# Where the weights and the token columns start in their rows: other start columns, and 258 + 256 in place of 256 + 258

## The chip, the cores and the metric

The kernel runs on one core of a Trainium2 chip. The metric is the time of one execution on the device, in microseconds (us); lower is better. Before the change three runs took 1018.99, 1019.06 and 1020.0 us, so the median is 1019.06 us.

A core has a matrix engine (TensorE, PE in the profile; PEld is its loading of weights), VectorE (DVE), ScalarE (ACT), GpSimd (POOL) and DMA queues, most of them fed by SyncE (SP). They run side by side and wait for one another by semaphores. Operands lie in a memory of 128 partitions; a "column" below is one fp32 value, 4 bytes, in every partition's row. TensorE accumulates in a memory of its own, which VectorE and ScalarE read.

## The reference

528 tokens (16 meta tokens and 512 real ones) of width 2048 are normalised, projected once into 65 tiles of 128 columns, and these feed two branches: a recurrence of 16 heads (r, k, v, a gate g, and two low-rank inputs), and a short gated convolution (B, C, h, a gate gc). The branches' outputs go through one output projection, the residual is added, and the result is normalised. In outline:

```python
hn = _rmsnorm(h_res, norm_in_g[l])
P = hn @ w_in[l]                                   # (528, 8320)
Pr, Pc = P[..., :RW_COLS], P[..., RW_COLS:]
prev = jnp.pad(Pr[:, :-1], ((0, 0), (1, 0), (0, 0)))
Pr = Pr + (prev - Pr) * mu_shift[l]                # token shift
r, k, v, g_r = ...                                 # 1024 columns each, then wl, al: 64 each
y = _rwkv7_recurrence(r, decay, k, v, kk, kk * a)
y_a = (groupnorm(y) + bonus) * jax.nn.silu(g_r)
Bg, Cg, hc, g_c = ...                              # 1024 columns each
y_b = Bg * _causal_depthwise_conv(Cg * hc, conv_w[l]) * jax.nn.silu(g_c)
h_res = h_res + jnp.concatenate([y_a, y_b], axis=-1) @ w_out[l]
out = _rmsnorm(h_res, norm_f_g)[:, N_META:]
```

The meta tokens are dropped at the end. So r and g_r, whose values are needed for the 512 real tokens but shifted by one, and C and h, which a convolution of width 3 reads, are needed for the real tokens and one or two before them; B and g_c for the real tokens alone; k and v for all 528.

## The kernel before

**The input projection.** The normalised input lies transposed in memory, in 16 rows of 576 columns each (`LX`), one row for every 128 of the 2048 input features; token t is at column t of a row. Each fp32 value is stored as a high part (`xh`) and a low part (`xl`), and the product is made of three matmuls: high weights times high x, high weights times low x, low weights times high x. For each of the 65 output tiles (8 each of k, v, r, g, C, h, B, gc, and one of the low-rank inputs, lora) the function `main` takes the weights in four quarters. A quarter holds four blocks of 128 x 128, and `steps` runs over the pieces of the token columns, the four blocks and the three products. Each matmul (line 326) has its own load of weights.

**The pieces.** Three constants say which token columns a tile computes: `FULL` (0 to 256 and 256 to 528; k, v, lora), `TAIL` (from 14, 514 columns in two pieces; r, g, C, h) and `REAL` (16 to 528 in one piece of 512; B, gc). So a tile of the first two kinds has 16 x 2 x 3 = 96 matmuls and one of the third 48. Each piece has a bank of the accumulator; `scaled` (line 345) copies it out on VectorE, multiplied by the tokens' scale, piece by piece.

**The weights' buffers.** A quarter of weights, 512 columns, comes by DMA, and `split_w` makes its high part (ScalarE, line 138) and low part (VectorE or GpSimd, line 139). They go into one of six buffers of 1088 columns: the high part begins at column `SHIFT[kind]`, the low part 512 columns behind it. The buffers are 17 x 64 columns long and the rows of x 9 x 64, so a start column's place within 64 columns is the same in every buffer and row.

**The order.** TensorE's order is written out by hand: a generator (`mains`) yields the projection's matmuls with an assumed duration of 0.43 ns a column, and the recurrence's preparation, inversion and steps call `fill` to put a given time's worth of them between their own small matmuls. Other engines are ordered by a scheduler. Until about 850 us TensorE works on the projection with the recurrence's work in between; behind it comes the output projection, seven products of a fast matrix multiplication (lines 1231 and 1433), with weights at column 40 of the same buffers or in places of their own.

Of the kernel before, what the change touches and what calls it, by code (L numbers as in the profile page):

```python
# [23 lines left out]
L = SEQ + META  # L24
# [50 lines left out]


LX = 576
SHIFT = {"lora": 16, "k": 16, "v": 32, "r": 30, "C": 30, "h": 62, "B": 16, "g": 30, "gc": 0, "out": 40}


@with_exitstack
def hymba_kernel(ctx: ExitStack, tc: tile.TileContext, xt, xtok, front, w_in, w_out, pv, lup, cst, msk, gf, out):
# [45 lines left out]
    def parts_of(kind, name):  # L128
        t = wp.tile([P, 2 * 512 + 64], F32R, tag="hl", name=name, bufs=6)
        o = SHIFT[kind]  # L130
        return t[:, o : o + 512], t[:, o + 512 : o + 1024]
# [45 lines left out]
    def tm(name):  # L177
        return tp.tile([P, LP], F32, tag="tm", name=name, bufs=3)
# [118 lines left out]
    with tc.issue_after(head):  # L297
        nc.vector.tensor_scalar(
            out=omm, in0=pvt[:, V_MU : V_MU + 33], scalar1=-1.0, scalar2=1.0, op0=ALU.mult, op1=ALU.add
        )  # L300
        for d, off in (
# [4 lines left out]
                out=d, in0=pvt[:, off : off + 8], scalar1=0.5, scalar2=None, op0=ALU.mult  # L306
            )
        nc.vector.tensor_scalar(
            out=hv[:, 4], in0=pvt[:, V_KA : V_KA + 8], scalar1=-0.5, scalar2=1.0, op0=ALU.mult, op1=ALU.add
# [1 line left out]

    nc.scalar.copy(ones, cs[:, C_BM : C_BM + P + 2])
    FULL = ((0, 256), (256, L))
    TAIL = ((14, 270), (270, L))
    REAL = ((META, L),)

    def steps(ps, ranges, k4, q, ks=range(4), rs_=range(2)):
# [13 lines left out]
    def banks(ranges, name, pool, tag):  # L331
        return [pool.tile([P, b - a], F32, tag=tag, name=f"ps_{name}_{r}") for r, (a, b) in enumerate(ranges)]

    def main(j, ranges, name):
        prefetch(2 * j + 4)
        ps = banks(ranges, name, pm, "main")
        for k4 in range(4):
            if k4 == 1:
                prefetch(2 * j + 5)
            yield from steps(ps, ranges, k4, 4 * j + k4)  # L340
        return ps

    def scaled(ranges, ps, dst, base):
        for (a, b), p in zip(ranges, ps):
            nc.vector.tensor_tensor(out=dst[:, a - base : b - base], in0=p, in1=rs[:, a:b], op=ALU.mult)
# [12 lines left out]
    def shift_real(ps, m, name, dst):  # L358
        pr = tp.tile([P, L + 1], F32, tag="pr", name=f"pr_{name}", bufs=2)
        scaled(TAIL, ps, pr, 14)  # L360
        sh = tm(f"sh_{name}")[:, 0:SEQ]
# [26 lines left out]
    def behind_of(what):  # L388
        return tc.issue_after(state.pop(what)) if what in state else nullcontext()

    def use(what, i, ps):
# [14 lines left out]
        elif what == "C":  # L406
            u = tm(f"u{i}")
            scaled(TAIL, ps, u, 14)
            got[what, i] = u
        elif what == "h":  # L410
            u = got["C", i]
            hh = tm(f"hh{i}")
            with behind_of("turned"):
                scaled(TAIL, ps, hh, 14)
            n = SEQ + 2
# [56 lines left out]
    def mains():  # L472
        pa = banks(FULL, "lora", pm, "main")
        pb = banks(FULL, "k0", pz, "tz")
        pc = banks(TAIL, "r0", pm, "main")
        pd = [pi.tile([P, SEQ], F32, tag="ser", name="ps_B0")]
        four = ((pa, FULL), (pb, FULL), (pc, TAIL), (pd, REAL))
        for k in range(4):
# [29 lines left out]
        for j in range(4, len(plan)):  # L508
            what, i = plan[j]
            rg = FULL if what in ("k", "v") else REAL if what in ("B", "gc") else TAIL  # L510
            ps = yield from main(j, rg, f"{what}{i}")
# [695 lines left out]
    def here(t, n):  # L1207
        return xa[t][:, n * 512 : (n + 1) * 512] if n < 2 else xb[n - 2][:, t]
# [147 lines left out]
    for u, unit in enumerate(units):  # L1356
        half, prod, g = unit
# [53 lines left out]
    with tc.manual_schedule(engines={mybir.EngineType.DVE, mybir.EngineType.Activation, mybir.EngineType.Pool}):  # L1411
# [16 lines left out]
        for part in range(2):  # L1428
# [7 lines left out]
            h = here(1, 2)[:, cols]  # L1436
# [70 lines left out]
```

## Time and profile before

| | |
|---|---|
| median of three runs | 1019.06 us |
| the profiled execution | 1019.06 us |
| its span, first to last instruction | 1017.3 us |
| TensorE busy | 1003.7 us, 9723 matmuls |
| VectorE / ScalarE / GpSimd busy | 675.5 / 393.5 / 270.6 us |
| mean granted clock of TensorE | 0.997 |

The page of the profile gives each engine's busy time and the chain of work that ended last, followed back from the last instruction. "Busy" for TensorE counts overlapping matmuls once: a matmul's own duration (some 0.28 us for 256 columns) is longer than the distance to the next one's start, since they are pipelined. The pace is therefore read from starts, or from the length of a long uninterrupted row of the chain, not from the durations. A row of the timeline has the start, the length, the engine, the line, what is written and read, the shape and the count.

### The profile page before, as it was taken

The numbers are of one execution on the slowest core, as the hardware profiler recorded it, in microseconds if no ns is written. First come the engines' busy times: TensorE is split into PE (matmuls) and PEld (weight loads), VectorE is DVE, ScalarE is ACT, GpSimd is POOL, SyncE is SP. The second block draws the span as 40 slices with busy tenths as digits, with TensorE's granted clock in tenths as the row PEclk, the third lists the DMA queues.
The fourth block names the chain that finished last, engine by engine and source line by source line (L and its number), as shares of the span: only waits on it lengthen the run. The fifth ranks groups of instructions, "written<-read, shape, count | busy, mean of one in ns | idle before, by whom it ended". The sixth has DMA issues, their size and how long they took to land.

```text
span 1017.3 us, 23682 instructions
## 1 busy us (share of the span) xinstructions
PE 1003.7 (99%) x9723; PEld 921.5 (91%) x9723; DVE 675.5 (66%) x1239; ACT 393.5 (39%) x729; POOL 270.6 (27%) x292
## 2 busy tenths in 40 slices
PE   9999999999999999999999999999999999999996
PEld 8999998999998999998999998889889898787875
DVE  7786855588665669554668553244555697998787
ACT  7553423344313434322434323222222335445453
POOL 0122514223123323222323222123332332015001
PEclk9999999999999999999999999999999999999998
DMA  9426485546665264853264746877663687695744
GB/s 324 152 82 152 134 210 147 149 124 164 163 158 164 91 168 104 211 148 117 85 178 108 200 139 185 295 224 226 222 206 94 186 272 193 171 327 134 177 124 166
DMA packets 185036, 174.82 MB, mean 172 GB/s; under 512 B 121568, under 2 KB 142816, under 8 KB 184416
## 3 DMA queue, kind: packets, MB, share of 16 engines
q1 hardware_dynamic: 182336, 164.40, 55.4%
q0 software_dynamic: 2304, 8.39, 4.7%
q8 instruction: 76, 1.25, 0.5%
q10 hardware_dynamic: 288, 0.52, 0.1%
q14 instruction: 32, 0.26, 0.1%
HBM read 136.92 MB, written 36.35 MB: 170 GB/s over the span
## 4 chain that ended last, share of the span: by engine, by line
PE 84%; DVE 9%; DMA 3%; issue 2%; ACT 1%; SPq 0%; POOL 0%; DVEq 0%; ACTq 0%; POOLq 0%
PE ps_v L326 9%; PE ps_g L326 9%; PE ps_k L326 9%; PE ps_h L326 9%; PE ps_r L326 9%; PE ps_B L326 9%; PE ps_gc L326 8%; PE ps_C L326 8%; DVE o L1204 3%; DMA wo<-in_w_out_dram 2%; PE g L671 2%; PE M L1231 2%; PE ps_lora L326 1%; PE zs L996 1%; PE zy L1000 1%
## 5 line engine op out<-in xcount | busy, mean ns | idle before, releaser
L138 ACT CAST w<-wr 128x512 fp32r<-128x512 f32 x252 | 153.3, 619 | 304.0 <-PE ps_C L326 53.0
L139 POOL TENSOR_TENSOR w<-wr,w 128x512 fp32r<-128x512 f32 x119 | 159.6, 1342 | 380.9 <-ACT w L138 315.6
L139 DVE TENSOR_TENSOR w<-wr,w 128x512 fp32r<-128x512 f32 x133 | 96.7, 733 | 112.2 <-ACT w L138 101.9
L326 PE MATMUL ps_v<-xh,w 128*128 128x272 f32 (+1 forms) x512 | 96.8, 286 | 0.0
L326 PE MATMUL ps_r<-xh,w 128*128 128x256 f32 (+1 forms) x512 | 96.7, 283 | 0.0
L326 PE MATMUL ps_h<-xh,w 128*128 128x258 f32 (+1 forms) x512 | 96.4, 285 | 0.0
L326 PE MATMUL ps_k<-xh,w 128*128 128x256 f32 (+1 forms) x512 | 95.7, 284 | 0.0
L326 PE MATMUL ps_C<-xh,w 128*128 128x258 f32 (+1 forms) x512 | 95.0, 284 | 0.0
L326 PE MATMUL ps_g<-xh,w 128*128 128x258 f32 (+1 forms) x512 | 93.5, 283 | 0.0
L326 PE MATMUL ps_B<-xh,w 128*128 128x512 f32 x256 | 83.4, 394 | 0.0
L326 PE MATMUL ps_gc<-xh,w 128*128 128x512 f32 x256 | 82.2, 396 | 0.2 <-DVE w L139 0.2
L326 PEld LDWEIGHTS ps_h<-xh,w 128*128 128x128 f32 x512 | 80.2, 189 | 1.1 <-issue 0.4
L326 PEld LDWEIGHTS ps_r<-xh,w 128*128 128x128 f32 x512 | 80.9, 189 | 0.3
L326 PEld LDWEIGHTS ps_v<-xh,w 128*128 128x128 f32 x512 | 80.3, 188 | 0.3
L326 PEld LDWEIGHTS ps_k<-xh,w 128*128 128x128 f32 x512 | 80.0, 189 | 0.5
L326 PEld LDWEIGHTS ps_C<-xh,w 128*128 128x128 f32 x512 | 79.9, 189 | 0.6
L326 PEld LDWEIGHTS ps_g<-xh,w 128*128 128x128 f32 x512 | 79.5, 189 | 0.3
L326 PE MATMUL ps_v<-xl,w 128*128 128x256 f32 (+1 forms) x256 | 73.1, 286 | 0.0
L326 PE MATMUL ps_h<-xl,w 128*128 128x256 f32 (+1 forms) x256 | 72.4, 283 | 0.3 <-issue 0.3
L326 PE MATMUL ps_k<-xl,w 128*128 128x256 f32 (+1 forms) x256 | 72.6, 283 | 0.0
L326 PE MATMUL ps_r<-xl,w 128*128 128x256 f32 (+1 forms) x256 | 72.5, 283 | 0.0
L326 PE MATMUL ps_g<-xl,w 128*128 128x256 f32 (+1 forms) x256 | 72.5, 283 | 0.0
(321 smaller groups left out, 2267.6 us busy)
## 6 DMA issues: line engine op xcount, KB each, us to landing
wr<-in_w_in_dram SPq DMA_DIRECT2D x126, 512.0 KB
ct<-opd SPq DMA_DIRECT2D x64, 288.0 KB
wo<-in_w_out_dram SPq DMA_DIRECT2D x24, 512.0 KB
x<-in_w_out_dram POOLq DMA_DIRECT2D x16, 512.0 KB, 6.0
opd<-ar SPq DMA_DIRECT2D x8, 576.0 KB
opd<-gt SPq DMA_DIRECT2D x16, 288.0 KB
opd<-bt SPq DMA_DIRECT2D x64, 64.0 KB
x<-in_w_out_dram SPq DMA_DIRECT2D x8, 512.0 KB
```

The source lines that it names most:

```text
L138: nc.scalar.copy(hi, rq)
L139: low[q] = eng.tensor_tensor(out=lo, in0=rq, in1=hi.bitcast(F32), op=ALU.subtract).ins
L326: nc.tensor.matmul(ps[r], ww[:, w], xx[:, kt, a:b], start=(kt == 0 and n == 0), stop=(kt == KT - 1 and n == 2))
L671: nc.tensor.matmul(z[h][:, c - c0], bk[hs, c, h : h + 2, :].rearrange("p a s -> p (a s)"), ar[hs, c].rearrange("p a s -> p (a s)"), start= ...
L996: nc.tensor.matmul(d[hs, j], w, x[hs], start=(a == 0), stop=(a == b - 1))
L1000: nc.tensor.matmul(d[ho, j], t[hs, o : o + CH], x[hs], start=(a == 0), stop=(a == b - 1))
L1204: nc.vector.tensor_tensor(out=lo, in0=rq, in1=hi.bitcast(F32), op=ALU.subtract)
L1231: nc.tensor.matmul(bank[s], left(prod, jj, m, s), w, start=(jj == 0 and n == 0), stop=(jj == 7 and n == 2))
```

## The change

Two constants change. The table of start columns, and the split of the 514 token columns:

```diff
-SHIFT = {"lora": 16, "k": 16, "v": 32, "r": 30, "C": 30, "h": 62, "B": 16, "g": 30, "gc": 0, "out": 40}
+SHIFT = {"lora": 16, "k": 16, "v": 16, "r": 32, "C": 64, "h": 32, "B": 16, "g": 32, "gc": 16, "out": 40}
...
     FULL = ((0, 256), (256, L))
-    TAIL = ((14, 270), (270, L))
+    TAIL = ((14, 272), (272, L))
     REAL = ((META, L),)
```

The weights of v move to column 16, where k's are; those of gc to 16, where B's are; those of r, g and h to 32; those of C to 64. For r, g, C and h the first piece is 14 to 272 (258 columns) and the second 272 to 528 (256 columns). What is computed, and the count of all instructions, stay the same.

## Prediction

> **What bounds the kernel now.** I read the page first (busy time per engine, then the chain that ended last), then the engines stage by stage, then what TensorE waits for, and last the chain and the timeline of single tiles, because the change touches only where TensorE reads. The page's busy times and its chain:
>
> ```profile
> span 1017.3 us, 23682 instructions
> PE 1003.7 (99%) x9723; PEld 921.5 (91%) x9723; DVE 675.5 (66%) x1239; ACT 393.5 (39%) x729; POOL 270.6 (27%) x292
> PE 84%; DVE 9%; DMA 3%; issue 2%; ACT 1%; SPq 0%; POOL 0%; DVEq 0%; ACTq 0%; POOLq 0%
> ```
>
> TensorE is busy for 99% of the span and carries 84% of the chain. Busy matmuls overlap, so this alone does not say that it is the limit. The view of stages (length, busy time and count for each engine, TensorE clock, DMA share, GB/s) and the view of TensorE's own waits say it:
>
> ```profile
> 0.00:53.00 53.00, 51.32 (x354) 46.47 (x355) 38.16 (x79) 33.45 (x66) 4.83 (x21) 1.00 0.70 235
> 53.00:150.00 97.00, 97.00 (x827) 95.43 (x826) 69.57 (x153) 40.54 (x75) 30.83 (x35) 1.00 0.55 143
> 700.00:850.00 150.00, 149.70 (x2002) 134.00 (x1998) 92.59 (x143) 45.76 (x85) 49.67 (x40) 1.00 0.68 202
> 850.00:1017.00 167.00, 156.05 (x698) 126.73 (x697) 143.83 (x208) 87.57 (x159) 28.50 (x30) 0.98 0.65 182
> ```
>
> ```profile
> PE M L1231 <- DVE o L1204: 1.7, 4, 0.7
> PE pwarm L187 <- DVE cold L184: 1.4, 1, 1.4
> PE rz L944 <- DMA ct<-opd: 0.2, 1, 0.2
> PE ps_gc L326 <- DVE w L139: 0.2, 1, 0.2
> ```
>
> From 53 to 850 us TensorE has no idle time worth a microsecond, at a granted clock of 1.00. Only behind 850 us, in the output projection, do 11 us stand open, and its VectorE is busy for 144 of 167 us. So a shorter input matmul (line 326) moves everything behind it forward, one for one, as long as the splits of the weights stay hidden. They do: TensorE waited 0.2 us for one of them, while ScalarE's cast, the first half of a split, waits for TensorE to free a buffer (columns: busy, mean ns of one, idle before it and what ended most of that):
>
> ```profile
> L138 ACT CAST w<-wr 128x512 fp32r<-128x512 f32 x252 | 153.3, 619 | 304.0 <-PE ps_C L326 53.0
> ```
>
> **How the pace depends on the column.** One tile is 96 matmuls in two pieces (k, v, r, g, C, h), or 48 in one piece of 512 (B, gc). The chain shows tiles that ran without interruption (start, length, count):
>
> ```profile
> 386.76 11.77 PE ps_v L326 x96
> 425.22 11.51 PE ps_C L326 x96
> 474.63 11.54 PE ps_k L326 x96
> 805.50 11.51 PE ps_C L326 x96
> 817.01 11.57 PE ps_h L326 x96
> 828.58 10.88 PE ps_B L326 x48
> 839.47 11.00 PE ps_gc L326 x48
> ```
>
> k and v read the same x columns (0 to 256 and 256 to 528), have equal counts and shapes, and differ in where the weights start in their buffer: column 16 against 32. The v tile takes 0.23 us more. B and gc both read x from column 16 in pieces of 512, with weights at 16 and at 0: gc takes 0.12 us more. So the position of the weights against x costs time, and it does so in the same way in buffers and rows whose bases differ by multiples of 64 columns (C takes 11.51 us at 425 and at 805 us).
>
> C has weights at 30 and x from 14 and from 270. Its 514 columns are 14 fewer than k's 528, yet it is only 0.03 us a tile faster. The timeline shows its two pieces beside k's. A low-half row (xl) stands for every third matmul, so the first to the fourth of a piece is nine matmuls:
>
> ```profile
> 477.45 0.28 PE L326 MATMUL ps_k<-xl,w 128*128 128x256 f32 x1
> 478.51 0.28 PE L326 MATMUL ps_k<-xl,w 128*128 128x256 f32 x1
> 478.87 0.28 PE L326 MATMUL ps_k<-xl,w 128*128 128x272 f32 x1
> 479.98 0.29 PE L326 MATMUL ps_k<-xl,w 128*128 128x272 f32 x1
> ```
>
> ```profile
> 428.05 0.28 PE L326 MATMUL ps_C<-xl,w 128*128 128x256 f32 x1
> 429.13 0.28 PE L326 MATMUL ps_C<-xl,w 128*128 128x256 f32 x1
> 429.49 0.28 PE L326 MATMUL ps_C<-xl,w 128*128 128x258 f32 x1
> 430.57 0.28 PE L326 MATMUL ps_C<-xl,w 128*128 128x258 f32 x1
> ```
>
> ```profile
> 819.86 0.28 PE L326 MATMUL ps_h<-xl,w 128*128 128x256 f32 x1
> 820.95 0.28 PE L326 MATMUL ps_h<-xl,w 128*128 128x256 f32 x1
> 821.30 0.29 PE L326 MATMUL ps_h<-xl,w 128*128 128x258 f32 x1
> 822.39 0.28 PE L326 MATMUL ps_h<-xl,w 128*128 128x258 f32 x1
> ```
>
> k: 1.06 / 9 = 117.8 ns for 256 columns and 1.11 / 9 = 123.3 ns for 272, so 16 columns cost 5.5 ns, about 0.35 ns each. C: 120.0 ns for 256 and 120.0 for 258. h: 121.1 and 121.1. Starts are given to 0.01 us, so a pace is good to about 1 ns. The same 256 columns are 2.2 ns dearer from column 14 (weights at 30) than from column 0 (weights at 16), though the distance, 16 columns, is equal: x that starts off a multiple of 16 costs something too.
>
> **The change part by part.** No instruction is added or removed, no DMA, no wait, no queue order. Buffers keep their 1088 columns (C's low half now ends at 64 + 1024, the last of them).
>
> (a) v from 32 to 16: exactly k's arrangement. 8 tiles x (11.77 - 11.54) = **-1.8 us**. The best known of the parts: the two rows differ in nothing else.
>
> (b) gc from 0 to 16: exactly B's arrangement. 8 x (11.00 - 10.88) = **-1.0 us**.
>
> (c) The second piece of r, g, C and h now reads x from 272, a multiple of 16, 256 columns instead of 258. For r, g and h the weights stand at 32, whose distance modulo 64 (272 is 16 more than a multiple of 64) is 16, which is k's first piece: 117.8 ns. r and g had C's arrangement, so C's 120.0 ns is taken for them: 48 matmuls x 8 tiles x 2.2 ns = 0.85 us each; h had 121.1: 384 x 3.3 = 1.27 us. For C the weights at 64 stand 48 columns from x modulo 64, which is gc's old place against x (0 against 16), the poor one of the two by the rows of gc and B. I take no gain there. Together 0.85 + 0.85 + 1.27 = **-3.0 us**. Bounds: no gain at all, and all four at 117.8, which is 3 x 0.85 + 1.27 = 3.8 us.
>
> (d) The first piece still starts at 14, with 258 columns, and weights at 32 (C: 64) instead of 30 (h: 62). No row shows weights on a multiple of 16 with x off it. What answers best for x is today's second piece (258 columns from 270, which is 14 modulo 64): 120.0 with weights at 30. From below the nearest row is k's 117.8, with two columns more, 118.5 ns. From above: position alone makes a difference of 2.4 ns a matmul between k and v (0.23 us / 96) and of 2.5 ns between B and gc (0.12 us / 48); that on top of 120.0 is 122.5. I take 119.3, between the lower end and today's second piece, because its x keeps that piece's place while the weights come to stand on a multiple of 16, as k's do. r, g and C: 384 x 3 x 0.7 = 0.8 us; h: 384 x 1.8 = 0.7 us. Together **-1.5 us**; bounds 1536 x (118.5 - 120.3) = -2.8 and 1536 x 2.2 = +3.4 us (120.3 being the mean of three at 120.0 and one at 121.1).
>
> (e) VectorE's scaling out of the accumulators takes 258 and then 256 columns instead of the reverse. The sum of the two is the same. The casts and subtractions write at other columns of the same buffer; they are hidden as shown above, and if one took some tens of ns longer it would cost nothing, for the buffer was freed several quarters earlier.
>
> (f) The order of TensorE's work is cut by a running sum of 0.43 ns a column. A first piece now counts 12 x 2 x 0.43 = 10 ns more and the second 10 ns less; a cut moves by one matmul at most. No wait is named above that stands within that distance; cost 0, and if it met the 0.2 us wait for a split, 0.2 us.
>
> Sum: 1.8 + 1.0 + 3.0 + 1.5 = 7.3 us. The profiled execution took 1019.06 us (span 1017.3 and 1.8 around it), which is the median of the three runs. 1019.1 - 7.3 = **1011.8 us**. What comes next to bind, behind 850 us, begins earlier by the same amount.
>
> [...]
>
> **The rivals.**
>
> Rival 1: column 32 is a dear column in itself, whatever x does. For it: v at 32 is dearer than k at 16 in both its pieces. Then r, g and h trade their 2.2 ns for v's 2.4 ns and gain nothing; only (a), (b) and a little of C and h remain: 1019.1 - 1.8 - 1.0 - 0.4 = 1015.9 us. Against it: with x from 14, weights at 30 pay 2.2 and weights at 62 pay 3.3 ns over k at 256 columns, so x off a multiple of 16 has a price at more than one column of the weights, and (c) takes it away.
>
> Rival 2, the other side: in the first piece, weights on a multiple of 16 and x 2 columns short of one meet in the same memory on every group of columns. Place: 1536 first-piece matmuls. It turns the whole change slower when it takes back the 5.8 us of (a) to (c) and 2 us more: 7.8 / 1536 = 5.1 ns a matmul, a pace of 125.4 ns. At 127 ns, say, the time is 1019.1 - 5.8 + 1536 x 6.7 / 1000 = 1023.6 us. For it: no row has this pairing, and gc shows that a mere shift can cost. Against it: the largest differences that position alone makes in the rows are the 2.4 and 2.5 ns above.
>
> Rival 3: the position of weights is not the cause, and v and gc are slower for another reason (their place in the order, what VectorE and GpSimd do beside them). Then nothing moves: 1019 us. Against it: gc and B, and C and h, ran back to back from 805 to 850 us under the same conditions and keep their difference. [...]
>
> **How the numbers follow.** The forecast, with (c) paying and (d) anywhere in its bounds: 0.66, from 1019.1 - 5.8 - 2.8 = 1010.5 (with C's second piece at 117.8 too, 1009.7) to 1019.1 - 5.8 + 3.4 = 1016.7 us. A further 0.06 goes to a larger gain than any row shows, down to 1006. Rival 1: 0.13. Rival 3: 0.07. Rival 2: 0.08. A difference under 0.2%, 2 us, can hardly be told from none; the three runs before spread over 1.0 us. Faster by more than that takes the forecast, the larger gain and most of rival 1 (1015.9 is 3.2 us): 0.66 + 0.06 + 0.11 = 0.83. Within: rival 3 and the rest of rival 1, 0.09. Slower: 0.08. From 1007 to 1017.5 us the range leaves out rivals 2 and 3 and the far end of the larger gain, 2 in 10.
>
> **What would show it.** In the chain of the changed kernel an uninterrupted v tile should take 11.54 us and a gc tile 10.88. In the timeline the 256-column piece of r, g and h should run at 117 to 118 ns and C's at about 120; the 258-column piece at 118.5 to 120. The stage from 53 to 850 us should show no new idle time of TensorE, and the projection's start should move forward by about 7 us. Wrong would be: a 258-column piece above 122 ns, v still at 11.77 us, or an equally early projection that ends no earlier.

## The result, and the profile after

The changed kernel takes 1011.11 us (median of five runs, 1009.72 to 1011.22) where the kernel before takes 1018.99 in the same series. The ratio is 0.9919, with a 95% interval from 0.9905 to 0.9932: 0.8% faster. The profiled execution took 1011.17 us, with a span of 1009.4 us. The page's busy times:

```profile
span 1009.4 us, 23682 instructions
PE 995.7 (99%) x9723; PEld 913.1 (90%) x9723; DVE 680.7 (67%) x1239; ACT 393.5 (39%) x729; POOL 285.9 (28%) x292
PE 85%; DVE 9%; DMA 3%; issue 2%; ACT 1%; POOL 0%; DVEq 0%; SPq 0%; ACTq 0%; POOLq 0%
```

TensorE has the same 9723 matmuls and 8.0 us less busy time; the shape of the page is otherwise unchanged, but for GpSimd (last section) and 5.2 us more of VectorE, 2.2 of them at line 139. The stages show where the time went. Each row is cut at about the end of the last projection tile, 850 us before and 842 us after. The row of the projection is 8 us shorter, with TensorE as full as before, and what follows takes 167 us in both. The first row is the kernel before, the other two are the changed kernel:

```profile
53.00:850.00 797.00, 796.29 (x8674) 748.33 (x8673) 493.45 (x953) 272.44 (x504) 237.29 (x241) 1.00 0.59 166
53.00:842.00 789.00, 788.75 (x8679) 741.13 (x8679) 499.40 (x956) 272.80 (x505) 252.60 (x241) 1.00 0.61 167
842.00:1009.00 167.00, 155.93 (x695) 126.04 (x693) 143.54 (x208) 87.20 (x159) 28.49 (x30) 0.99 0.66 183
```

Uninterrupted tiles of the chain (start, length, count), to be held against the same tiles of the kernel before:

```profile
383.63 11.54 PE ps_v L326 x96
421.44 11.20 PE ps_C L326 x96
470.20 11.58 PE ps_k L326 x96
797.19 11.39 PE ps_C L326 x96
808.58 11.29 PE ps_h L326 x96
819.87 10.90 PE ps_B L326 x48
830.77 10.90 PE ps_gc L326 x48
```

v has k's old 11.54 us, and gc has B's pace. C is at 11.20 or 11.39 us instead of 11.51, h at 11.29 instead of 11.57. The last gc tile ends at 830.77 + 10.90 = 841.67 us; before it was 839.47 + 11.00 = 850.47. So 8.8 us were gained by the end of the projection, of which the span keeps 7.9. The timeline of the C tile shows both pieces:

```profile
424.20 0.28 PE L326 MATMUL ps_C<-xl,w 128*128 128x258 f32 x1
425.28 0.28 PE L326 MATMUL ps_C<-xl,w 128*128 128x258 f32 x1
425.63 0.28 PE L326 MATMUL ps_C<-xl,w 128*128 128x256 f32 x1
426.65 0.28 PE L326 MATMUL ps_C<-xl,w 128*128 128x256 f32 x1
```

The first piece keeps its pace, 1.08 / 9 = 120.0 ns. The second falls from 120.0 to 1.02 / 9 = 113.3 ns.

Below, "mean pace" is the mean distance of starts within a kind's pieces over the whole trace, interruptions left out. By it the parts of the change come to:

| | before, ns | after, ns | matmuls | us |
|---|---|---|---|---|
| v, 256 and 272 columns | 118.9, 126.5 | 116.8, 123.7 | 384 each | -1.9 |
| gc, 512 | 229.5 | 227.6 | 384 | -0.7 |
| second pieces of r, g, C, h | 119.8, 119.7, 119.8, 120.7 | 115.9, 115.8, 115.3, 115.4 | 384 each | -6.8 |
| first pieces of r, g, C, h | 120.5, 120.0, 120.0, 120.3 | 120.2, 120.3, 119.7, 120.6 | 384 each | 0.0 |
| k, first piece (untouched) | 116.9 | 117.6 | 384 | +0.3 |

The sum is -9.1 us, against 8.8 read at the end of the projection. (B, also untouched, rose by 0.5 ns, 0.2 us, and is not in the table.)

### The profile page after: what moved, and what is told of

Its sections match the earlier page's. It is cut to its first block, busy times and chain, and to the rows that moved or that the text cites. A ratio compares the mean times of both kernels' runs of the same rounds, so it can differ in the third digit from the quotient of the medians.

```text
span 1009.4 us, 23682 instructions
## 1 busy us (share of the span) xinstructions
PE 995.7 (99%) x9723; PEld 913.1 (90%) x9723; DVE 680.7 (67%) x1239; ACT 393.5 (39%) x729; POOL 285.9 (28%) x292
## 4 chain that ended last, share of the span: by engine, by line
PE 85%; DVE 9%; DMA 3%; issue 2%; ACT 1%; POOL 0%; DVEq 0%; SPq 0%; ACTq 0%; POOLq 0%
PE ps_k L326 9%; PE ps_v L326 9%; PE ps_h L326 9%; PE ps_C L326 9%; PE ps_g L326 9%; PE ps_r L326 9%; PE ps_B L326 9%; PE ps_gc L326 8%; DVE o L1204 3%; DMA wo<-in_w_out_dram 2%; PE g L671 2%; PE M L1231 2%; PE ps_lora L326 1%; PE zs L996 1%; PE zy L1000 1%
## 5 line engine op out<-in xcount | busy, mean ns | idle before, releaser
L139 POOL TENSOR_TENSOR w<-wr,w 128x512 fp32r<-128x512 f32 x119 | 174.9, 1470 | 360.6 <-ACT w L138 308.0
L139 DVE TENSOR_TENSOR w<-wr,w 128x512 fp32r<-128x512 f32 x133 | 98.9, 750 | 105.8 <-ACT w L138 104.1
L326 PE MATMUL ps_r<-xh,w 128*128 128x258 f32 (+1 forms) x512 | 95.2, 281 | 0.0
L326 PE MATMUL ps_h<-xh,w 128*128 128x256 f32 (+1 forms) x512 | 94.6, 283 | 0.0
L326 PE MATMUL ps_C<-xh,w 128*128 128x256 f32 (+1 forms) x512 | 93.2, 281 | 0.0
L326 PE MATMUL ps_g<-xh,w 128*128 128x256 f32 (+1 forms) x512 | 92.1, 281 | 0.0
L326 PE MATMUL ps_g<-xl,w 128*128 128x258 f32 (+1 forms) x256 | 72.3, 282 | 0.0
L326 PE MATMUL ps_r<-xl,w 128*128 128x258 f32 (+1 forms) x256 | 72.1, 282 | 0.0
L326 PE MATMUL ps_h<-xl,w 128*128 128x258 f32 (+1 forms) x256 | 71.9, 281 | 0.0
```

Of the source, the lines that this page charges most:

```text
L139: low[q] = eng.tensor_tensor(out=lo, in0=rq, in1=hi.bitcast(F32), op=ALU.subtract).ins
L326: nc.tensor.matmul(ps[r], ww[:, w], xx[:, kt, a:b], start=(kt == 0 and n == 0), stop=(kt == KT - 1 and n == 2))
```

## The experiments

Three theories of the second piece's gain stood at the start. X: where x starts decides. W: where the weights start decides. P: both have to stand well. The first three runs do one part of the change each; all times are medians beside runs of the kernel before on the same chip (1019.1 us here).

**v and gc alone.**

```diff
-SHIFT = {... "v": 32, ... "gc": 0, ...}
+SHIFT = {... "v": 16, ... "gc": 16, ...}
```

> The kernel before with only two start columns changed: v's weights at 16 and gc's at 16. If the place of the weights against x sets the pace, an uninterrupted v tile falls from 11.77 to 11.54 us and a gc tile from 11.00 to 10.89, and the time falls by 8 x 0.23 + 8 x 0.11 = 2.7 us, to about 1016.3. If v and gc were slow for another reason (their place in the order, other engines' work), both tiles keep their length and the time stays within 1 us of the kernel before.

1016.47 us, ratio 0.9976 (0.9965 to 0.9986), as expected. The chain:

```profile
385.94 11.53 PE ps_v L326 x96
803.61 11.51 PE ps_C L326 x96
826.69 10.88 PE ps_B L326 x48
837.58 10.90 PE ps_gc L326 x48
```

v and gc move to the paces of k and B, and C does not move. Nothing but their weights' start columns was changed, so that v and gc were slow for another reason is excluded.

**The pieces alone.**

```diff
-    TAIL = ((14, 270), (270, L))
+    TAIL = ((14, 272), (272, L))
```

> The kernel before with only the pieces changed: 14 to 272 and 272 to 528, all weights where they were (r, C, g at 30, h at 62). Theory X (where x starts decides): the second piece gets the pace seen after, about 115.5 ns, the first stays at 120; 384 x 4 x 4.4 ns = 6.8 us less, about 1012.3 us. Theory W (where the weights start decides): the second piece stays at 119 to 120 ns and the time within 1.5 us of the kernel before. Theory P (both must stand on a multiple of 16): as W for the pieces' pace, since the weights stay off it.

1016.51 us, ratio 0.9970 (0.9959 to 0.9981). A C tile takes 11.41 us; its 256-column piece, of which the first and fourth low-half rows follow, 1.06 / 9 = 117.8 ns:

```profile
428.73 0.28 PE L326 MATMUL ps_C<-xl,w 128*128 128x256 f32 x1
429.79 0.29 PE L326 MATMUL ps_C<-xl,w 128*128 128x256 f32 x1
```

The mean pace of the four second pieces is 117.9 ns: neither X's 115.5 nor the 119 to 120 of W, which P expected here too.

**The weights of r, g, h and C alone.**

```diff
-SHIFT = {... "r": 30, "C": 30, "h": 62, ... "g": 30, ...}
+SHIFT = {... "r": 32, "C": 64, "h": 32, ... "g": 32, ...}
```

> The kernel before with only the weights of r, g, h at 32 and of C at 64; pieces as before (14 to 270, 270 to 528), v and gc as before. Theory W (the weights' column decides): the second piece, 258 columns from 270, falls from 120 to about 116 ns; some 6 us less, about 1013 us. Theories X and P (x must start on a multiple of 16, for P the weights too): both pieces stay at 119 to 121 ns and the time within 1.5 us of the kernel before.

1018.72 us, ratio 0.9998 (0.9989 to 1.0007): no difference. The second pieces stay at 119.7 ns; in the C tile below 1.08 / 9 = 120.0:

```profile
426.95 0.28 PE L326 MATMUL ps_C<-xl,w 128*128 128x258 f32 x1
428.03 0.28 PE L326 MATMUL ps_C<-xl,w 128*128 128x258 f32 x1
```

So W is out. The columns are worth nothing while the piece is wrong and another 2.4 ns once it is right (117.9 to 115.5). P comes nearest, as an interaction, but in the form on record it missed the 117.9. The columns also changed the distance between weights and x from 14 to 16 modulo 64 (for r, g and C's old column 30), so the distance may be what counted. The three parts gain 2.6, 2.6 and 0.4 us by the medians, together 5.6; the change gains 7.9.

**Earlier starts of the first piece.** The open point was now the first piece, which had gained nothing.

```diff
+STARTS = {"r": 14, "g": 12, "C": 8, "h": 0}
...
+    def tail(kind):
+        return ((STARTS[kind], 272), (272, L))
```

> The changed kernel with the first piece begun earlier for three of the four kinds: r from 14 as it is (258 columns), g from 12 (260), C from 8 (264), h from 0 (272); the columns in front of 14 are computed and not used. At 0.42 ns a column beyond 256 and the pace of the second piece (115.5 ns), a start that is good enough gives 117.2 ns from 12, 118.8 from 8 and 122.2 from 0, against 120.2 from 14. If a group of 4 columns (16 bytes) is enough: g gains 384 x 3 = 1.2 us, C 384 x 1 = 0.4 us, h loses 0.9 us: about 0.7 us less than the changed kernel, 1010.4. If only a multiple of 16 columns counts: g about 121 and C about 122.7 ns, and with h at 123 the time is 384 x (0.8 + 2.7 + 2.6) = 2.3 us more, 1013.4 us.

1012.29 us, ratio 0.9934 (0.9919 to 0.9949), 1.2 us above the changed kernel's own median. g from 12, with 260 columns, takes 120.0 ns as before; C from 8 with 264 columns 122.1; h from 0 with 272 columns 126.6. Neither list of expected paces came out. The 0.42 ns a column in them was an estimate: in the changed kernel's table above, v's two pieces lie (123.7 - 116.8) / 16 = 0.43 ns a column apart, and k's, of 117.6 and 123.5 ns, 0.37. h is instructive: x from 0 and weights at 32 are the distance that v had, and the price is v's old one (126.5 for 272 columns), while k, with weights at 16, does 272 columns in 123.5. A second surprise: the second pieces, of which nothing was changed, ran at 113.6 to 114.0 ns behind the longer first pieces, against 115.5.

**Other distances of the weights.**

```diff
-SHIFT = {... "k": 16, "v": 16, "r": 32, "C": 64, "h": 32, "B": 16, "g": 32, "gc": 16, ...}
+SHIFT = {... "k": 0, "v": 48, "r": 48, "C": 32, "h": 64, "B": 32, "g": 16, "gc": 48, ...}
```

> The changed kernel with the weights at other distances from x, all on multiples of 16. Distance modulo 64 (weights minus x): k 0, v 48, B 16, gc 32, second pieces of r 32, g 0, C 16, h 48. If the distance alone decides, as v and gc suggest, 32 is dear (v before: 118.9 ns for 256 and 126.5 for 272 columns, h from column 0 in the run with earlier starts: 126.6 for 272): gc rises from 227.6 to about 230 ns and r's second piece from 115.9 to about 118. 16 is good: B stays or falls below 228, C keeps 115.3. 48 was good for C's 256 columns and poor for gc's 512, so v at 48 tells: 116.8 and 123.7 if it is good, about 118 and 126 if not. 0 was good for B: k keeps 117.6 and 123.5 and g 115.8. Time: 384 x (2.4 + 2.1) = 1.7 us more than the changed kernel, about 1012.8 us. If instead any multiple of 16 is as good as another, nothing moves: 1011 us.

1018.66 us, ratio 0.9989 (0.9980 to 0.9998): almost the whole gain is gone, and much more than the 1.7 us expected, although all the weights stand on multiples of 16 and no start of x was moved. The chain:

```profile
474.30 11.72 PE ps_k L326 x96
537.98 11.73 PE ps_v L326 x96
828.19 11.19 PE ps_B L326 x48
839.38 11.18 PE ps_gc L326 x48
```

So the place of the weights matters, but not by one rule for all lengths. In mean paces, by the distance (start of the weights minus start of x) modulo 64, for x that starts on a multiple of 16 (this run, the changed kernel and the kernel before):

| distance | 0 | 16 | 32 | 48 |
|---|---|---|---|---|
| 256 columns | 118.9 to 119.4 | 115.4 to 117.6 | 118.5 to 118.9 | 115.3 to 117.8 |
| 272 columns | 125.6 | 123.5 | 126.5 | 126.2 |
| 512 columns | 228 | 233.1 | 232.4 | 229.5 |

For 256 columns 16 and 48 are the good ones; for 512 columns 0 is, and 16, the best for k, is the worst. For 256 columns it is the distance and not the column in itself: weights at 32 cost v 118.9 ns with x from 0, and h 115.4 ns with x from 272. For 272 and for 512 columns x stood at one place modulo 64 in all these runs, so there the two can't be told apart.

**First piece from 12 for all four kinds.**

```diff
-    TAIL = ((14, 272), (272, L))
+    TAIL = ((12, 272), (272, L))
```

> The changed kernel with the first piece of all four kinds from 12 instead of 14 (260 columns, two of them unused). In the run with earlier starts g's pieces from 12 took 120.0 and 114.0 ns against 120.3 and 115.8. If that carries over to r, C and h, the time falls by 1536 x 2.0 = 3 us, to about 1008 us. If g's gain came from the tiles in front of it, which also began earlier, r, C and h keep 120.2 and 115.5 (plus up to 0.8 ns for two more columns) and the time stays at 1011 to 1012 us.

1010.82 us, ratio 0.9916 (0.9900 to 0.9933): not to be told from the changed kernel. r, g and h have 114.2 to 114.5 ns in the second piece, but C rose from 115.3 to 116.7 there.

**Both pieces begun on a multiple of 16.** Tokens 14 and 15 are copied behind the last one, so that the second piece holds them.

```diff
+    for x in (xh, xl):
+        nc.vector.tensor_copy(x[:, :, L : L + 2], x[:, :, 14:16])
...
+    BOTH = ((16, 272), (272, L + 2))      # for r (but the first), g, C, h
```

> The changed kernel with both pieces begun on a multiple of 16: tokens 14 and 15 are copied behind the last token (columns 528 and 529 of each row of x), and the pieces are 16 to 272 (256 columns) and 272 to 530 (258), for all but the first r tile; a small VectorE operation puts the two columns in front. If the start of x on a multiple of 16 is what the first piece lacked (theory P), the two pieces take 113.4 to 117.8 and 114.2 to 118.6 ns in place of 120.2 and 115.5: with the means of these, 231.9 in place of 235.7, 31 x 48 x 3.8 = 5.6 us less, about 1005.5 us (999 to 1012 by the two ends). If the first piece's 120 came from its odd number of columns beyond 256, the 258 columns take 120 wherever they stand and the 256 columns 115.5: no gain, 1011 to 1012 us.

1010.84 us, ratio 0.9913 (0.9898 to 0.9928): no gain over the changed kernel. The timeline of an h tile says why:

```profile
811.42 0.28 PE L329 MATMUL ps_h<-xl,w 128*128 128x256 f32 x1
812.45 0.28 PE L329 MATMUL ps_h<-xl,w 128*128 128x256 f32 x1
812.78 0.28 PE L329 MATMUL ps_h<-xl,w 128*128 128x258 f32 x1
813.87 0.29 PE L329 MATMUL ps_h<-xl,w 128*128 128x258 f32 x1
```

256 columns from 16 take 1.03 / 9 = 114.4 ns, but 258 columns from 272, a multiple of 16, take 1.09 / 9 = 121.1. The dear price has only changed places. It belongs neither to the start alone (258 columns cost 120 from 14 and from 272) nor to the count alone (256 columns cost 120 from 14, and 113 to 118 from 16 or 272). What the dear ones share is called theory G from here on: they reach into one group of columns more than 256 aligned ones do. Two separate prices, one for the start and one for the count, remain possible, but then 258 columns from 14 would have to pay only one of them.

**Weights half a group of 16 off.**

```diff
+SHIFT = {... "k": 24, "v": 8, "r": 40, "C": 56, "h": 8, "B": 24, "g": 24, "gc": 8, ...}
```

> The changed kernel with every kind's weights half a group of 16 columns off: k 24, v 8, B 24, gc 8, r 40, g 24, C 56, h 8. Theory G (a matmul pays for each group of 16 columns that its reads touch; x of 256 columns from 272 touches 16, of 258 from 14 or from 272 touches 17): 128 weights off a multiple of 16 touch 9 groups instead of 8, so every piece pays about what the weights at 30 and 62 paid in the run with the pieces alone (118 ns against 115.5 in the second piece): 2.4 ns x 4600 two-piece matmuls and as much for B and gc, some 12 us more, about 1023 us. If only the distance counts, and smoothly, each piece lies between its neighbours at multiples of 16 (k between 117.6 and 118.9, and between 123.5 and 125.6; v between 116.8 and 118.9; B and gc between 228 and 233; g's second piece between 115.8 and 119.4): about 3.5 us more, 1014.6 us.

1019.18 us, ratio 0.9996 (0.9986 to 1.0006), between the two expectations. k at 24 keeps 117.5 and 124.0 ns, although its weights stand off a multiple of 16; B and gc rise to 233 ns, and in the second piece r and g to 118.7 and 118.3, h to 117.6 and C to 119.5. A group of 16 does not explain the weights, since k would have risen too. Only the weights were moved, so their place again decides, and not smoothly with the distance.

**How wide is a group?** 256 columns from 12 and from 8.

```diff
+STARTS = {"r": 12, "g": 12, "C": 8, "h": 8}
-SHIFT = {... "r": 32, "C": 64, "h": 32, "g": 32, ...}
+SHIFT = {... "r": 28, "C": 24, "h": 24, "g": 28, ...}
...
+        return ((a, a + 256), (a + 256, L))      # a = STARTS[kind]
```

> The changed kernel with 256 columns in the first piece of every two-piece tile of r, g (12 to 268, weights at 28) and C, h (8 to 264, weights at 24), so that the distance of the weights stays 16; the second pieces are 268 to 528 (260 columns) and 264 to 528 (264). Theory G says that a piece pays about 5 ns more as soon as its x reaches into one group of columns more than its count needs. If the group is 16 columns, 256 columns from 12 or from 8 touch 17 and cost 120 ns, as 256 from 14 did; both pieces stand at 120 to 122 and the time is 1536 x 5 = 7 us above the changed kernel, 1018 us. If the group is 4 columns, 12 and 8 are as good as 16: the first piece costs 113.4 to 118 ns, the second 120 (260) and 122 (264), and the time is 1011 to 1013 us. If it is 8 columns, C and h do the one and r and g the other.

1012.57 us, ratio 0.9939 (0.9920 to 0.9959), in the place expected for groups of 4. A C tile, with its first piece from 8:

```profile
424.29 0.28 PE L331 MATMUL ps_C<-xl,w 128*128 128x256 f32 x1
425.34 0.28 PE L331 MATMUL ps_C<-xl,w 128*128 128x256 f32 x1
425.68 0.28 PE L331 MATMUL ps_C<-xl,w 128*128 128x264 f32 x1
426.79 0.28 PE L331 MATMUL ps_C<-xl,w 128*128 128x264 f32 x1
```

256 columns from 8 take 1.05 / 9 = 116.7 ns (mean 115.7), and from 12 a mean of 116.3, where from 14 they had taken 120.0. So a start on a multiple of 4 columns, 16 bytes, is good enough, and 14, a multiple of 2, is not. Leaving aside the run with the weights half a group off, and with the weights 16 or 48 columns from x, or at most 8 off that, 64 groups of four cost 113 to 118 ns, 65 groups (256 from 14, 258, 260) 119 to 121, and 66 groups (264) 122. At the distances 0 and 32 even 64 groups cost 118.5 to 119.4, as the table above has it. The 514 columns from 14 to 528 lie in 129 groups of four, so one of two pieces has 65 at least, and the changed kernel is at that floor. The run also says what the columns did in the first three: here neither the weights (24, 28) nor x (8, 12) stand on a multiple of 16, only their distance is 16, and the pace is near the changed kernel's 115.5. So theory P's multiples of 16 are not needed. Column 30 with x from 272 lacked two things, the distance of 16 and a multiple of 4 for the weights. The second alone is not enough, as r's 118.7 ns in the run half a group off shows (weights at 40); whether it is needed beside the distance was not tested.

**The changed kernel again, and a version that leaves C at 14.**

> The changed kernel once more, beside the version below on the same chip: 1011 us, ratio to the kernel before about 0.992.

1010.94 us, ratio 0.9916 (0.9902 to 0.9929). The mean paces repeat to 0.1 ns, and the tiles' two lengths too (C at 11.20, later 11.38 us).

```diff
+STARTS = {"r": 12, "g": 12, "C": 14, "h": 12}
...
+        return ((STARTS[kind], 272), (272, L))
```

> The changed kernel with the first piece of r, g and h from 12 (260 columns) and C's from 14 as it is. In the run with all four from 12, r, g and h took 120.0 + 114.4 ns for the two pieces where the changed kernel took 120.4 + 115.7, and C 119.2 + 116.7 where it took 119.7 + 115.3. If a kind's pace depends on its own pieces alone, 384 x 3 x 1.7 = 2.0 us less than the changed kernel, 1009 us. If it also depends on what runs in front of it (the same C tile has been seen at 11.20 and 11.39 us), the gain is anything from 0 to 3 us and C's pieces change though nothing of C is changed.

1010.97 us, ratio 0.9915 (0.9902 to 0.9929): no difference. r, g and h kept a gain of 1 to 1.7 ns in the second piece, but the first C tile, of which nothing was changed, went from 11.20 us to 11.38. The first row is the changed kernel, the other two are this run with its first two C tiles:

```profile
132.08 11.20 PE ps_C L326 x96
131.29 11.38 PE ps_C L330 x96
270.79 11.20 PE ps_C L330 x96
```

v's first piece went from 116.8 to 117.2 ns. So a piece has more than one pace for the same operands, and something outside of it decides which one it takes. What ran in front of it is the likeliest; this run changed that, and with it the timing of the other engines. No version was found that is measurably faster than the changed kernel.

## Why the prediction was right, and where it was not

The forecast of 1011.8 us and its range held; the median was 1011.1. Two of its steps came near their numbers and two missed in opposite directions. Part of the agreement is this cancellation, which was luck, and so is the 0.9 us that the span did not keep of the larger gain.

(a) v: -1.8 forecast, -1.9 by the mean paces; 11.54 us a tile, as its row said. (b) gc: -1.0 forecast, -0.7. The gc row that was used, 11.00 us, was right, and B came to 10.90 rather than 10.88. The run with these two alone confirms both.

(c) The second pieces: -3.0 forecast, -6.8 measured. Mechanism right, size wrong, in two terms. For r, g and h the price was k's 117.8 ns, read from a single piece, but 256 columns in the good position run at 113.3 or at 117.8 ns, and these kinds came to 115.4 to 115.9. For C no gain was taken, because 48 columns of distance were poor for gc's 512 columns. That transfer failed: C's second piece has 115.3 ns, and the table of distances shows that 48 is good for 256 columns and poorer than 0 for 512.

(d) The first piece: -1.5 forecast, 0.0 measured. The sentence that failed is the choice of 119.3 because "the weights come to stand on a multiple of 16". The weights' column is worth nothing here: 258 columns from 14 take 119.9 ns with the old weights (the pieces alone) and 120.2 with the new ones. The piece pays for its 65th group of four columns, wherever it starts (119 to 121 ns, where 64 groups took 113 to 118 with the weights within 2 of 16 or 48 columns from x), and "a multiple of 16" was too coarse: a multiple of 4 does for x (256 columns took 116.3 ns from 12, 115.7 from 8). Its nearest row, the old second piece at 120.0, would have been the better forecast.

(e) Casts and subtractions in other columns: hidden, as forecast, though GpSimd's grew by 15 us in all (below). (f) The moved cuts cost nothing visible. One price was missing: k's first piece, whose operands were not touched, rose from 116.9 to 117.6 ns, 0.3 us. It came with v and gc rather than with the pieces: the run with v and gc alone has 117.5, the one with the pieces alone 117.0. The cause was not found.

"One for one" behind 850 us was nearly right: of 8.8 us the span kept 7.9. From the last gc tile to the end the profile has 166.8 us before and 167.7 after, and 167.1 in the repeated run with the same end of the projection, so some of the 0.9 us varies between executions; where it arises was not settled.

Rival 1, column 32 as dear in itself, falls: r, g and h stand there at 115.5 ns. Rival 2, a collision in the first piece, did not come: 120.2 ns. Rival 3, another reason for v and gc, is excluded by the run with these two alone. With x and all shapes unchanged, moving B's weights from a distance of 0 to 16 columns took its tile from 10.90 to 11.19 us, so the weights' place has a price.

The width of a group that fits the runs is 4 columns of 4 bytes, 16 bytes: with the weights 16 columns from x, 256 columns took 115.7 ns from column 8 and 116.3 from 12, and r, g and C 120.0 to 120.5 from 14 before the change. What in the hardware makes it so is not shown.

## What to carry to other kernels

In this kernel fp32r matmuls of 256 columns, each with its own weights, followed one another without a gap, and their pace depended, among other things, on the columns where x and the weights start: the means went from 113.6 ns to 120.5. What to try elsewhere: keep the columns read to as few 16-byte groups as their count needs (65 groups took 119 to 121 ns, 64 with the weights 16 or 48 columns from x 113 to 118), and try the weights' start column modulo 64 for each length of piece on its own, since a distance of 16, good for 256 columns (115.4 to 117.6 ns), was the worst of the four tried at multiples of 16 for 512 (233.1). Look at the pace between starts, since the duration of a matmul (0.28 or 0.29 us in all the rows above) does not show it. And take a price from the mean of many pieces: one piece may stand in the slower of two paces, as C's second piece did at 117.8 ns against 113.3.

## What was not expected

A piece has several steady paces with equal operands. In the changed kernel C's second piece ran at 113.3 ns in the tiles up to 571 us and at 117.8 in most later ones; the run that left C's own pieces alone moved the first C tile from one to the other. The C tile that starts at 743.58 us even changed within itself. Its second quarter takes 1.02 / 9 = 113.3 ns in the second piece; then matmuls of the recurrence come between, and the third quarter takes 1.06 / 9 = 117.8:

```profile
746.90 0.28 PE L326 MATMUL ps_C<-xl,w 128*128 128x256 f32 x1
747.92 0.28 PE L326 MATMUL ps_C<-xl,w 128*128 128x256 f32 x1
750.99 0.28 PE L326 MATMUL ps_C<-xl,w 128*128 128x256 f32 x1
752.05 0.28 PE L326 MATMUL ps_C<-xl,w 128*128 128x256 f32 x1
```

What sets the pace in the hardware was not found.

GpSimd's half of the split became slower. In the view of line 139 (count, then minimum, median and maximum in ns), before and after:

```profile
L139 POOL TENSOR_TENSOR w<-wr,w x119: 1082/1282/4147, 60.2 to 838.6; 128x512 fp32r<-128x512 f32 x119
```

```profile
L139 POOL TENSOR_TENSOR w<-wr,w x119: 1264/1292/4403, 60.5 to 831.2; 128x512 fp32r<-128x512 f32 x119
```

Before, the undisturbed subtractions for r, g, C and h, with columns 30 and 62, took 1.09 us and those for the other kinds 1.28; after the change all take at least 1.26. The start columns do it: the run with the pieces alone keeps the 1.09 us (minimum 1.084), the one with the columns alone has none under 1.27. With an input and an output two columns off a multiple of 4 this engine took 1.09 us here, and on one 1.26 or more. It stays hidden: TensorE waits 0.2 us for a subtraction after the change, as before.

```profile
PE ps_gc L326 <- DVE w L139: 0.2, 1, 0.2
```

Where GpSimd is the limit, the old columns might be the better ones; that was not tried.
